# Weight sums in DRAM by smaller groups from the output projection on, later x forms, one gate block more in plain form, and another order of the second phase

## The chip, the core and the metric

One core of a Trainium2 chip runs the kernel. TensorE (PE; its weight loads are the row PEld), VectorE (DVE), ScalarE (ACT), GpSimd (POOL) and SyncE (SP) work from instruction queues of their own, each in its own order, and wait for one another at semaphores. SP, ACT and POOL also issue DMA transfers. The metric is the device time of one execution in microseconds, the median of several runs.

## What is computed

One layer on x of 512 tokens by 1024 features, in float32:

```python
h = rms_norm(x, norm_mix_g)
cb, cc, cin, q, k, v, f_logit, g_logit = split(h @ w_in)
y_conv = (cb * causal_dwconv(cc * cin, conv_mix_w)) @ w_out_conv
y_attn = forgetting_attention(q, k, v, cumsum(log_sigmoid(f_logit + b_f))) @ w_out_attn
g_conv, g_attn = split(sigmoid(g_logit + b_gate))
x = x + (g_conv * y_conv + g_attn * y_attn) @ w_o
a, b = split(causal_dwconv(rms_norm(x, norm_ffn_g) @ w_up, conv_ffn_w))   # 2816 wide each
x = x + (silu(a) * b) @ w_down
return rms_norm(x, norm_f_g)
```

## The kernel before

Features lie on the 128 partitions and tokens along the free axis, so x is 8 blocks (kb) of 128 by 512. Each weight chunk is 128 by up to 1024: eight 128x128 tiles, one per block of the contraction. To keep float32 accuracy, each operand is split into a high part, rounded to the PE's format (ACT, L250, names wh_...), and the low rest (DVE, L254, names wl_...). A product is three passes: high x high, low x high, high x low (mm3, L281). A plain block, one output block of 128 features, is 8 tiles x 3 passes x 2 halves of the tokens = 48 matmuls.

**Chunks and queues.** `stream` lists all weight chunks in the order of their use. `load` issues a chunk's DMA on SP into one of four buffers (`raw`; further ones for F chunks), a few chunks ahead; `split` makes the two parts, in two buffers of each kind; `chunk` hands them to the matmuls. A buffer is loaded again once its last split is done, so SP's queue runs some blocks ahead of PE. Small pieces of work wait in the list `later`, each with a chunk number from which it may run and a cost in us; `run_later`, at the end of every `split`, issues as many as a budget for the chunk allows, and `flush` forces those that a matmul is about to need.

**Seven-product steps.** For the gate weights of blocks j from GJ on, and for most of the down projection, 2x2 groups of tiles are multiplied with seven products in place of eight (`seven`, matmuls at L299). A step (i, q) is a pair of output blocks i and a pair of contraction blocks q. Two steps make a double, listed in GATES (gates) and STEPS (down projection, first and second phase). A double has 2 x 7 x 3 = 42 matmuls and two chunks: P with six tiles that are read as they are, F with eight tiles that are sums of weights. The input side needs sums too: `x_sums` and `x_split` make those of x for the gates (tiles xt, xth, xtl), the closures t13, t24 and hl in `glu` those of the hidden layer (tiles ge, go, gh, gl).

**Weight sums in DRAM.** The sums for F are made by DMA alone, from one DRAM tensor (`wst`) to a DRAM tile f, for a group of doubles at a time (`make_forms`). Six operations in a chain per group: a plain copy (SP, L194), an accumulating copy (POOL, L197), a copy of a part of f (SP), an accumulating copy (POOL), again a copy (SP) and an accumulating copy (POOL). A copy from f waits for the sum before it. `GROUPS` gives for each of the three sets the doubles per group, the slots between two operations of a chain, and the slots by which the next group's chain is shifted. A slot is a call of `slot()`: one per unit of attention, and one per up block; there `todo_bg` operations that are due are issued, and so take their place in SP's and POOL's queues between the loads and the vector work that are issued there.

**Order of the program.** v projection; q and k; attention units mixed with the remaining projections (here the gates' sums are made); then for each j of 8 the two gates and the mix block (conv and attention output); output projection wo0 to wo7; first phase: 24 up blocks (pairs j = 0 to 11, each evacuated by DVE and ACT and multiplied on POOL, L1026 and L1033), then the 12 doubles of STEPS[0]; second phase: 20 up blocks and the doubles of STEPS[1]; at last two output blocks in plain form (chunks dp0 to dp2, tile pdA and others) and the final norm. In the second phase i = 2 goes on in PSUM from the first phase (HELD), i = 0 takes the banks X and i = 1 the banks Y, which i = 2 holds before. The pair q = 10 comes from the last up blocks.

Of the kernel before, what the change touches and what calls it, by code (L numbers as in the profile page):

```python
# [10 lines left out]
AF = mybir.ActivationFunctionType  # L11
# [23 lines left out]
G1, G2, GF, BG, CM, CF, BF = 0, 8, 16, 24, 40, 52, 184  # L35
# [10 lines left out]
STEPS = (  # L46
    tuple(((i, q), (i, q + 1)) for i, q in ((0, 0), (0, 2), (1, 0), (1, 2), (0, 4), (1, 4)))
    + tuple(((i, q), (i, q + 1)) for i in (3, 2) for q in (0, 2, 4)),
    (((2, 6), (2, 7)), ((2, 8), (2, 9)), ((2, 10), (0, 6)), ((0, 7), (0, 8)), ((0, 9), (0, 10)))
    + (((1, 6), (1, 7)), ((1, 8), (1, 9)), ((1, 10),)),  # L50
)
HELD = 2

GJ = 2
GATES = tuple(((j, q), (j, q + 1)) for j in range(GJ, KB) for q in (0, 2))

PLAIN = [(m, k) for m in (6, 7) for k in range(*PHASES[1])]
PCUTS = (0, 8, 12, 20)

DOUBLES = GATES + STEPS[0] + STEPS[1]  # L60
GROUPS = {"gate": (2, 4, 1), 0: (4, 2, 4), 1: (4, 2, 3)}


@with_exitstack
def block_kernel(ctx, tc, xT, vecs, wv, win, wmix, wo, wup, wst, wdp, outT):
# [3 lines left out]
    nc = tc.nc  # L69
# [6 lines left out]
    def keep(ins):  # L76
        return tc.keep_in_program_order(ins)
# [16 lines left out]
    def col(i):  # L94
        return vec[:, i : i + 1]
# [22 lines left out]
    stream = [(f"v{kb}", wv[kb], S + H) for kb in range(KB)]  # L118
    stream += [wi(i) for i in early + late]
    n = 0  # L120

    def step_chunks(n):
        m = len(DOUBLES[n])
        return [(f"P{n}", wst[n, :, : 3 * m * P], 3 * m * P), (f"F{n}", n, 4 * m * P)]

    for j in range(KB):
        if j >= GJ:
            stream += step_chunks(n) + step_chunks(n + 1)
# [13 lines left out]
    raws, parts, order = [], [], {}  # L142
    pools = {"raw": wp}
    later = []
# [33 lines left out]
    def make_forms(n0, n1, key):  # L178

        size, step, shift = GROUPS[key]  # L180
        cuts = [n0]
        for n in range(n0 + 1, n1 + 1):
            if n == n1 or n - cuts[-1] == size or len(DOUBLES[n]) != len(DOUBLES[cuts[-1]]):
                cuts.append(n)
        for g, (a, b) in enumerate(zip(cuts, cuts[1:])):
            m = len(DOUBLES[a]) * P
            f = dr.tile([P, b - a, 4 * m], F32, tag=f"f{a}", name=f"f{a}")
            w = wst[a:b].rearrange("n p c -> p n c")
            x0, x1, x2 = w[:, :, 3 * m : 5 * m], w[:, :, 5 * m : 7 * m], w[:, :, 7 * m : 8 * m]
            for n in range(a, b):  # L190
                made[n] = f[:, n - a, :]

            def put(dst, src):
                return lambda: keep(nc.sync.dma_start(dst, src))  # L194

            def add(dst, src):
                return lambda: keep(nc.gpsimd.dma_start(dst, src, accum_op=ALU.add))  # L197

            f0, f1, f2 = f[:, :, : 2 * m], f[:, :, 2 * m : 3 * m], f[:, :, 3 * m :]
            ops = (put(f0, x0), add(f0, x1), put(f1, f[:, :, :m]), add(f1, x1[:, :, m:]), put(f2, f1), add(f2, x2))  # L200
            todo_bg.extend((make_forms.slot + step * k + shift * g, op) for k, op in enumerate(ops))
        todo_bg.sort(key=lambda w: w[0])

    make_forms.slot = 0

    def slot():

        while todo_bg and todo_bg[0][0] <= make_forms.slot:
            todo_bg.pop(0)[1]()
        make_forms.slot += 1  # L210
# [20 lines left out]
    def split(hl=None):  # L231

        k = len(parts)
        if k == len(stream):
            return
        nm, _, ncol = stream[k]
        load(k + (LOOK if len(raws) > KB else AHEAD))
        if hl is None:
            hl = []
            for x in "hl":  # L240
                if k == 0:
                    wp.tile([P, PADW[x]], F32, tag=f"pad{x}", name=f"pad_{x}")
                hl.append(wp.tile([P, D], F32R, tag=f"w{x}", name=f"w{x}_{nm}", bufs=2)[:, :ncol])
        hi, lo = hl
        raw = raws[k]
        if k == 0:
            for cs in (slice(0, VW), slice(VW, S + H)):
                keep(nc.vector.tensor_copy(hi[:, cs], raw[:, cs]))
        else:
            ins = nc.scalar.activation(hi, raw, AF.Copy)  # L250
            order["hi"] = ins.ins
            if k < KB:
                keep(ins)
        ins = nc.vector.tensor_sub(lo, raw, hi.bitcast(F32))  # L254
        order["lo"] = ins.ins
        if k < KB:
            keep(ins)
        held[tag_of(k)] -= 1
        parts.append((hi, lo))
        run_later(k, {"u": 1.7, "P": 1.6, "F": 0.75, "i": 3.0, "m": 3.0}.get(nm[0], 3.5))  # L260
# [380 lines left out]
    n = 4 * H  # L641
# [62 lines left out]
    for idx in late:  # L704
        kind, i = divmod(idx, 4)
# [7 lines left out]
    n = len(units)  # L713
# [22 lines left out]
    th = [slice(0, 2 * P), slice(2 * P, S)]  # L736

    def split_next():
        if len(parts) == chunk.n and not stream[chunk.n][0].startswith("dp"):
            split()  # L740

    open_ = {}
# [41 lines left out]
    xt = xp.tile([P, KB, S], F32, tag="x1", name="xt")  # L784
# [23 lines left out]

    for q in range(4):
        nc.gpsimd.dma_start(xt[:, 2 * q : 2 * q + 2, :], xT[:, 2 * q : 2 * q + 2, :])  # L810
        for kb in (2 * q, 2 * q + 1):
            nc.scalar.activation(xt[:, kb, :], xt[:, kb, :], AF.Copy, scale=col(G1 + kb))
    xq = xt.rearrange("p (q b) (h c) -> p q (b h) c", b=2, h=2)
    xqh, xql = (t.rearrange("p (q b) (h c) -> p q (b h) c", b=2, h=2) for t in (xth, xtl))

    def x_sums(qs):
        b11, b12, b21, b22 = (xq[:, qs, i, :] for i in range(4))

        def f():
            nc.vector.tensor_sub(b11, b11, b12)  # L820
            nc.vector.tensor_sub(b12, b22, b12)

        def g():
            nc.vector.scalar_tensor_tensor(b22, b11, -1.0, b22, op0=ALU.mult, op1=ALU.subtract)
            nc.vector.scalar_tensor_tensor(b21, b22, -1.0, b21, op0=ALU.mult, op1=ALU.subtract)

        return f, g
# [5 lines left out]

        return f

    k = [c[0] for c in stream].index("mix0")
    for q in (0, 2):
        f, g = x_sums(slice(q, q + 2))
        later.append((k, 1.4, (("q", q),), f))
        later.append((k, 1.5, (("q", q),), g))  # L840
        for i in (q, q + 1):
            later.append((k + 1, 1.25, (("q", i),), x_split(i)))
        k += 2
# [49 lines left out]
    for j in range(KB):  # L893
        gs = []
        if j == 0:
            evac_gate(0, gs)(gp[0])
            evac_gate(8, gs)(gp[1])
        elif j < GJ:
            run_all(proj(20 + j, f"ga{j}", evac_gate(j, gs), acc))
            run_all(proj(28 + j, f"gb{j}", evac_gate(8 + j, gs), acc))  # L900
        else:
            if j == GJ:
                acc = ring(2, 7, 3, 4)
            seven(GATES[2 * (j - GJ) : 2 * (j - GJ) + 2], 2 * (j - GJ), {j: (0, 1, 5, 6)}, gate_form, done=gate_pair(j, gs))
        wh, wl = chunk(f"mix{j}")
        yc, ya = acc(f"yc{j}"), acc(f"ya{j}")
        for pp, hh, ll, o in ((yc, ych, ycl, 0), (ya, oth, otl, 4)):
            for k in range(4):
                ks = slice((o + k) * P, (o + k + 1) * P)
                mm3(pp, wh[:, ks], wl[:, ks], hh[:, k, :], ll[:, k, :], k == 0, k == 3)  # L910
        if j >= GJ:
            split_next()
# [57 lines left out]
        return q  # L970

    po = None
    for j in range(KB):
        if j == 0:
            po = lead(["wo0", "wo1"], mh, ml)
        p = po[j] if j < 2 else block(f"wo{j}", mh, ml)
        xr = mt(f"xr{j}")
        nc.gpsimd.dma_start(xr, xT[:, j, :])
        nc.vector.tensor_add(x1[:, j, :], p, xr)
        nc.scalar.activation(x1h[:, j, :], x1[:, j, :], AF.Copy, scale=col(G2 + j))  # L980
        nc.vector.scalar_tensor_tensor(
            x1l[:, j, :], x1[:, j, :], col(G2 + j), x1h.bitcast(F32)[:, j, :],
            op0=ALU.mult, op1=ALU.subtract,
        )
        square_into(ssq2, x1[:, j, :], j == 0, mp, f"sq2_{j}")
# [126 lines left out]
    for ph, (j0, j1) in enumerate(PHASES):  # L1112
        if ph:
            flush()
            acc = ring(*X)
        n = len(GATES) + ph * len(STEPS[0])
        make_forms(n, n + len(STEPS[ph]), ph)
        for j in range(j0, j1):
            pu = None
            if j == 0:  # L1120
                nrm = {}

                def mid():
                    nrm["c"] = rstd_col([ssq2], NT, 6, "n2")

                def late():
                    nrm["b"] = rstd_sb(rstd_bc(nrm["c"], NT, 7, "n2"), "n2")

                pu = lead(["up0", "up1"], x1h, x1l, mid, late)
            glu(ph, j, up(j, nrm["b"], pu))  # L1130
        assert not todo_bg
        seven(
            STEPS[ph], len(GATES) + ph * len(STEPS[0]), ({0: X, 1: Y, 3: X, 2: Y}, {0: X, 1: Y, 2: Y})[ph],
            lambda q, g: (gh[:, place(ph, q) + g, :], gl[:, place(ph, q) + g, :]),
            goes_on=HELD if ph == 1 else None, stays=HELD if ph == 0 else None,
            done=lambda i, banks, ids: combine(ph, i, banks, ids),
        )
# [175 lines left out]
```

## Time and profile before

| | us |
|---|---|
| median of three runs | 737.57 (732.33 to 738.46) |
| the profiled execution | 735.92 |
| its span, first to last instruction | 734.1 |
| PE busy in it | 705.7 |
| DVE, ACT, POOL busy | 498.0, 338.5, 163.9 |
| mean granted PE clock | 0.984 |

The profile gives each engine's busy time, a list of who waited for whom (idle time of an engine, put down to what released it last), and busy times in any stretch of the span, with the clock that PE was granted there and the share of time that the 16 DMA engines were busy. Lines such as L250 belong to the helpers, so tiles tell the places apart: p_up is an up block, dn a seven-product step, p_ga and p_gb the two gates in plain form. In the table the span of one execution stands beside that execution's own time; the sums of the prediction are made against the latter.

### The profile page before, as it was taken

To read this page: it belongs to the slowest core of one execution; us is meant where nothing else is said; L and a number is where in the kernel's file an instruction comes from. 1 tells how busy PE (TensorE), PEld (TensorE's weight loads), DVE (VectorE), ACT (ScalarE), POOL (GpSimd) and SP (SyncE) were. 2 spreads that over 40 slices of the span, in tenths; PEclk is the share of its full clock that TensorE was granted. 3 is DMA by queue.
4 is the path that set the end of the run, shared out by engine and by line. 5 is a ranking of instruction groups with operands and counts; after the bars stand their busy time and mean duration, and the time that the engine had idled before them with its cause. 6 is when DMAs were issued, how large, how long until landed. Compare 5 with 4: busy or idle time off the path is not lost. (4 is left out here: it accounts for less than half of the span.)

```text
span 734.1 us, 14600 instructions
## 1 busy us (share of the span) xinstructions
PE 705.7 (96%) x6042; PEld 700.8 (95%) x6042; DVE 498.0 (68%) x773; ACT 338.5 (46%) x528; POOL 163.9 (22%) x177
## 2 busy tenths in 40 slices
PE   9999999999898999999999798999999999999996
PEld 9999999999898999999998698999999999998985
DVE  6687767556288778844385485877684687878683
ACT  6574545434455444434253243445443344445552
POOL 5124856522100000222222032210000213210002
PEclk9999999999999999999999989999999999999998
DMA  7428989542523555452447986774656489554313
GB/s 264 145 69 283 233 220 194 129 87 65 208 60 122 187 188 178 144 171 89 144 74 209 264 150 185 213 214 150 193 163 215 76 227 251 148 174 153 98 30 114
DMA packets 54130, 118.91 MB, mean 162 GB/s; under 512 B 4624, under 2 KB 24080, under 8 KB 54064
## 3 DMA queue, kind: packets, MB, share of 16 engines
q1 hardware_dynamic: 38320, 96.00, 40.5%
q0 software_dynamic: 14336, 20.75, 16.4%
q10 hardware_dynamic: 1408, 1.24, 0.5%
q8 instruction: 47, 0.77, 0.4%
q14 instruction: 19, 0.16, 0.1%
HBM read 115.80 MB, written 35.13 MB: 206 GB/s over the span
## 5 line engine op out<-in xcount | busy, mean ns | idle before, releaser
L281 PE MATMUL p_up<-x1h,wh_up 128*128 128x256 f32 x536 | 105.8, 279 | 0.0
L281 PE MATMUL p_up<-x1h,wl_up 128*128 128x256 f32 x536 | 105.7, 279 | 0.0
L281 PE MATMUL p_up<-x1l,wh_up 128*128 128x256 f32 x536 | 105.3, 278 | 0.0
L250 ACT ACTIVATE wh_up<-raw_up 128x1024 fp32r<-128x1024 f32 x44 | 46.6, 1058 | 96.8 <-PE p_up L281 54.6
L254 DVE TENSOR_TENSOR wl_up<-raw_up,wh_up 128x1024 fp32r<-128x1024 f32 x44 | 55.6, 1264 | 42.6 <-ACT wh_up L250 42.6
L281 PEld LDWEIGHTS p_up<-x1h,wh_up 128*128 128x128 f32 x536 | 82.1, 191 | 0.0
L281 PEld LDWEIGHTS p_up<-x1h,wl_up 128*128 128x128 f32 x536 | 82.1, 190 | 0.0
L281 PEld LDWEIGHTS p_up<-x1l,wh_up 128*128 128x128 f32 x536 | 81.7, 190 | 0.0
L1026 POOL TENSOR_TENSOR ge<-fu,fu 128x512 f32<-128x512 f32 x11 | 17.0, 1550 | 194.9 <-DVE fu L531 182.0
L281 PE MATMUL p_in<-xgh,wh_in 128*128 128x256 f32 x288 | 56.9, 279 | 1.0 <-ACT wh_in L250 1.0
L281 PE MATMUL p_in<-xgl,wh_in 128*128 128x256 f32 x288 | 56.5, 277 | 0.0
L281 PE MATMUL p_in<-xgh,wl_in 128*128 128x256 f32 x288 | 56.4, 277 | 0.0
L254 DVE TENSOR_TENSOR wl_F<-raw_F,wh_F 128x1024 fp32r<-128x1024 f32 (+1 forms) x32 | 43.7, 1365 | 14.8 <-ACT wh_F L250 14.8
L299 PE MATMUL p_up<-x1h,wh_up 128*128 128x256 f32 x168 | 41.4, 282 | 10.2 <-ACT wh_up L250 10.2
L250 ACT ACTIVATE wh_F<-raw_F 128x1024 fp32r<-128x1024 f32 (+1 forms) x32 | 33.7, 1052 | 32.9 <-PE dn L299 26.6
L197 POOL DMA_DIRECT2D f<-in_wst_dram x36 | 47.3, 1436 | 0.1
L1013 DVE TENSOR_TENSOR fz<-p_up,rb_n 128x512 f32<-128x512 f32 x44 | 30.2, 689 | 24.6 <-PE p_up L281 24.6
L281 PEld LDWEIGHTS p_in<-xgh,wh_in 128*128 128x128 f32 x288 | 44.7, 188 | 1.9 <-ACT wh_in L250 1.2
L281 PEld LDWEIGHTS p_in<-xgl,wh_in 128*128 128x128 f32 x288 | 43.6, 188 | 0.0
L281 PEld LDWEIGHTS p_in<-xgh,wl_in 128*128 128x128 f32 x288 | 43.5, 188 | 0.0
L299 PEld LDWEIGHTS p_up<-x1h,wh_up 128*128 128x128 f32 x168 | 32.1, 191 | 10.8 <-ACT wh_up L250 10.8
L250 ACT ACTIVATE wh_P<-raw_P 128x768 fp32r<-128x768 f32 (+1 forms) x32 | 26.6, 832 | 31.1 <-PE dn L299 22.7
(306 smaller groups left out, 2079.8 us busy)
## 6 DMA issues: line engine op xcount, KB each, us to landing
raw_up<-in_wup_dram SPq DMA_DIRECT2D x44, 512.0 KB, 5.6
raw_F<-f SPq DMA_DIRECT2D x31, 512.0 KB, 4.3
raw_in<-in_win_dram SPq DMA_DIRECT2D x24, 512.0 KB, 3.6
raw_P<-in_wst_dram SPq DMA_DIRECT2D x31, 384.0 KB, 4.2
f<-in_wst_dram POOLq DMA_DIRECT2D x14, 512.0 KB, 8.8
raw_mix<-in_wmix_dram SPq DMA_DIRECT2D x8, 512.0 KB, 6.6
raw_wo<-in_wo_dram SPq DMA_DIRECT2D x8, 512.0 KB, 4.1
f<-in_wst_dram SPq DMA_DIRECT2D x4, 1024.0 KB, 5.9
```

What stands on the lines that cost most here:

```text
L197: return lambda: keep(nc.gpsimd.dma_start(dst, src, accum_op=ALU.add))
L250: ins = nc.scalar.activation(hi, raw, AF.Copy)
L254: ins = nc.vector.tensor_sub(lo, raw, hi.bitcast(F32))
L281: keep(nc.tensor.matmul(out[:, cs], w, x[:, cs], start=start and i == 0 and c == 0, stop=stop and i == 2 and c == len(cut) - 1,))
L299: keep(nc.tensor.matmul(out, wl if x == 1 else wh, xl if x == 2 else xh, start=opens and bk not in seen, stop=closes and bk not in left,))
L1013: nc.vector.tensor_mul(z, p, rb2)
L1026: keep(nc.gpsimd.tensor_mul(ge, a.rearrange(halves_of, h=2), b.rearrange(halves_of, h=2)))
```

## The change

- **GROUPS** gives the two phases groups of two doubles. First phase: four slots between operations in place of two, a shift of one in place of four. Second phase: three in place of two, a shift of one in place of three. Chains: six for three in the first phase, five for three in the second.
- The first phase's chains start with the output projection, which now calls `slot()` too: eight slots more. The slot count starts at 0 with every call of `make_forms`.
- **x forms**: the scaling of x by the norm's weight (ACT) was issued right behind the DMAs of x, ahead of everything that followed; it is now put in `later`, to run from the split of the chunk mix1 on, and the sums likewise from mix1 in place of mix0.
- **GJ = 3**: the gates of block 2 are computed in plain form (two plain blocks of 48 matmuls in place of two doubles of 42), and there are ten gate doubles in place of twelve.
- **STEPS[1]**, the second phase's order: the pair of steps with (2, 10) comes one double later, and the single step moves from the end to the sixth place.
- `split_next` may also split dp0 ahead.

```diff
-    (((2, 6), (2, 7)), ((2, 8), (2, 9)), ((2, 10), (0, 6)), ((0, 7), (0, 8)), ((0, 9), (0, 10)))
-    + (((1, 6), (1, 7)), ((1, 8), (1, 9)), ((1, 10),)),
+    (((2, 6), (2, 7)), ((2, 8), (2, 9)), ((0, 6), (0, 7)), ((0, 8), (2, 10)), ((0, 9), (0, 10)))
+    + (((1, 6),), ((1, 7), (1, 8)), ((1, 9), (1, 10))),
...
-GJ = 2
+GJ = 3
...
-GROUPS = {"gate": (2, 4, 1), 0: (4, 2, 4), 1: (4, 2, 3)}
+GROUPS = {"gate": (2, 4, 1), 0: (2, 4, 1), 1: (2, 3, 1)}
...
     def make_forms(n0, n1, key):
 
         size, step, shift = GROUPS[key]
+        make_forms.slot = 0
...
-    make_forms.slot = 0
...
     def split_next():
-        if len(parts) == chunk.n and not stream[chunk.n][0].startswith("dp"):
+        if len(parts) == chunk.n and stream[chunk.n][0] not in ("dp1", "dp2"):
             split()
...
     for q in range(4):
         nc.gpsimd.dma_start(xt[:, 2 * q : 2 * q + 2, :], xT[:, 2 * q : 2 * q + 2, :])
-        for kb in (2 * q, 2 * q + 1):
-            nc.scalar.activation(xt[:, kb, :], xt[:, kb, :], AF.Copy, scale=col(G1 + kb))
...
+    def x_scale(q):
+        def f():
+            for kb in (2 * q, 2 * q + 1):
+                nc.scalar.activation(xt[:, kb, :], xt[:, kb, :], AF.Copy, scale=col(G1 + kb))
+
+        return f
...
-    k = [c[0] for c in stream].index("mix0")
+    k = [c[0] for c in stream].index("mix1")
     for q in (0, 2):
         f, g = x_sums(slice(q, q + 2))
+        for i in (q, q + 1):
+            later.append((k, 0, (("q", i),), x_scale(i)))
         later.append((k, 1.4, (("q", q),), f))
...
     po = None
+    make_forms(len(GATES), len(GATES) + len(STEPS[0]), 0)
     for j in range(KB):
+        slot()
         if j == 0:
             po = lead(["wo0", "wo1"], mh, ml)
...
         if ph:
             flush()
             acc = ring(*X)
-        n = len(GATES) + ph * len(STEPS[0])
-        make_forms(n, n + len(STEPS[ph]), ph)
+        if ph:
+            make_forms(len(GATES) + len(STEPS[0]), len(DOUBLES), ph)
```

**ACT at the gates.** ACT's queue from the last projection of the attention stage on: g are the gates' sigmoids, wh_in29 the split of the second gate's chunk of block 1, xt the scaling of x (L812 before, L816 now), xth the forms' high part. Before:

```order
L802 ACTIVATE g0_2609<-g0_2609,vec_64 128x512
L802 ACTIVATE g8_2612<-g8_2612,vec_64 128x512
L812 ACTIVATE xt_2589<-xt_2589,vec_64 128x512 x4
L250 ACTIVATE wh_in29_2725<-raw_in29_2392 128x1024
L812 ACTIVATE xt_2589<-xt_2589,vec_64 128x512 x4
```

And now:

```order
L801 ACTIVATE g0_2594<-g0_2594,vec_64 128x512
L801 ACTIVATE g8_2597<-g8_2597,vec_64 128x512
L249 ACTIVATE wh_in29_2706<-raw_in29_2385 128x1024
L924 ACTIVATE mh_2588<-g0_2594 128x512
L249 ACTIVATE wh_mix1_2712<-raw_mix1_2476 128x1024
L816 ACTIVATE xt_2582<-xt_2582,vec_64 128x512 x4
L801 ACTIVATE g1_2724<-g1_2724,vec_64 128x512
L249 ACTIVATE wh_in22_2780<-raw_in22_2545 128x1024
L835 ACTIVATE xth_2583<-xt_2582 128x1024 x2
```

The eight scalings moved from ahead of and around the split of in29 to behind the split of mix1 (four of them) and, not shown, behind that of in30.

**SP in the first up blocks.** SP's queue at the start of the first phase: raw_up are the up chunks' loads, f<-in_wst_dram a chain's first copy, f<-f a copy that waits for a sum. Before:

```order
L170 DMA raw_up4_4503<-in_wup_dram 128x1024
L194 DMA f12_4494<-in_wst_dram 512x1x512
L170 DMA raw_up5_4640<-in_wup_dram 128x1024
L170 DMA raw_up6_4701<-in_wup_dram 128x1024
L194 DMA f12_4494<-f12_4494 512x256
L194 DMA f16_4495<-in_wst_dram 512x1x512
L170 DMA raw_up7_4767<-in_wup_dram 128x1024
```

And now:

```order
L170 DMA raw_up4_4499<-in_wup_dram 128x1024
L195 DMA f10_3972<-f10_3972 256x256
L195 DMA f12_3973<-f12_3973 256x256
L195 DMA f14_3974<-f14_3974 256x256
L170 DMA raw_up5_4639<-in_wup_dram 128x1024
L195 DMA f16_3975<-f16_3975 256x256
L170 DMA raw_up6_4701<-in_wup_dram 128x1024
L195 DMA f18_3976<-f18_3976 256x256
L170 DMA raw_up7_4767<-in_wup_dram 128x1024
```

The first copies have left this place for the output projection; the copies from f are half as large, and one stands between two loads.

**DVE at the start of the second phase's steps.** wl_P26 and wl_F26 before, wl_P25 and wl_F25 now, are the low parts of the chunks of the double that holds (2, 10); go10 and gl are the sums of q = 10 and their low parts. Before:

```order
L254 TENSOR_TENSOR wl_P26_8237<-raw_P26_8052,wh_P26_8236 128x768
L1047 SCALAR_TENSOR_TENSOR go10_8120<-go10_8120 128x256
L1053 TENSOR_TENSOR gl_4492<-ge10_7983,gh_4491 128x2x256
L1048 SCALAR_TENSOR_TENSOR go10_8120<-go10_8120 128x256
L1053 TENSOR_TENSOR gl_4492<-go10_8120,gh_4491 128x512 x2
L254 TENSOR_TENSOR wl_F26_8275<-raw_F26_8054,wh_F26_8274 128x1024
L1053 TENSOR_TENSOR gl_4492<-go10_8120,gh_4491 128x512
```

And now:

```order
L253 TENSOR_TENSOR wl_P24_8255<-raw_P24_8070,wh_P24_8254 128x768
L1055 SCALAR_TENSOR_TENSOR go10_8138<-go10_8138 128x256
L1061 TENSOR_TENSOR gl_4491<-ge10_7999,gh_4490 128x2x256
L1056 SCALAR_TENSOR_TENSOR go10_8138<-go10_8138 128x256
L253 TENSOR_TENSOR wl_F24_8287<-raw_F24_8072,wh_F24_8286 128x1024
L1061 TENSOR_TENSOR gl_4491<-go10_8138,gh_4490 128x512
L253 TENSOR_TENSOR wl_P25_8319<-raw_P25_8139,wh_P25_8318 128x768
L1061 TENSOR_TENSOR gl_4491<-go10_8138,gh_4490 128x512 x2
L253 TENSOR_TENSOR wl_F25_8347<-raw_F25_8141,wh_F25_8346 128x1024
```

The three low parts of go10 stood behind the P chunk of the double that needs them; now one stands ahead of that chunk, and a whole double (P24, F24) that does not need them lies before.

## The prediction

> **What bounds the kernel now.** I read the busy times first, then what TensorE (PE) waits for, then stretches of 15 us, then the queues behind the waits. On the page:
>
> ```profile
> PE 705.7 (96%) x6042; PEld 700.8 (95%) x6042; DVE 498.0 (68%) x773; ACT 338.5 (46%) x528; POOL 163.9 (22%) x177
> ```
>
> PE is busy 96% of the span, so only two things can be gained: matmuls, and the few stretches in which PE stands still or runs slowly. The list of PE's waits names nearly all of the standing still (line; released by; us, times, longest):
>
> ```profile
> PE p_up L299 <- ACT wh_up L250: 10.2, 3, 5.5
> PE p_gb L281 <- ACT wh_in L250: 2.1, 1, 2.1
> PE pdA L281 <- DVE wl_dp L254: 1.6, 2, 0.8
> PE dn L299 <- DVE gl L1053: 1.4, 1, 1.4
> PE dn L299 <- ACT xth L831: 1.2, 1, 1.2
> PE dn L299 <- DVE xtl L832: 1.0, 2, 0.9
> PE p_gb L281 <- DVE wl_in L254: 0.8, 1, 0.8
> ```
>
> The stretches give the places and a second loss, the clock (columns: stretch, length, busy us and count of PE, PEld, DVE, ACT, POOL, then PE clock, DMA share, GB/s):
>
> ```profile
> 195.00:210.00 15.00, 12.14 (x93) 11.74 (x92) 8.31 (x10) 9.55 (x13) 1.21 (x1) 0.89 0.55 186
> 210.00:225.00 15.00, 12.33 (x101) 11.57 (x100) 12.56 (x15) 7.68 (x9) 1.29 (x1) 1.00 0.28 87
> 240.00:255.00 15.00, 15.00 (x134) 15.00 (x134) 11.86 (x16) 7.08 (x9) 1.30 (x1) 1.00 0.49 156
> 390.00:405.00 15.00, 13.22 (x113) 12.82 (x112) 9.84 (x13) 6.58 (x9) 3.92 (x3) 1.00 0.64 173
> 405.00:420.00 15.00, 11.51 (x102) 11.31 (x100) 6.82 (x13) 3.25 (x5) 1.30 (x1) 1.00 0.92 251
> 420.00:435.00 15.00, 13.00 (x91) 13.00 (x92) 10.96 (x14) 6.69 (x9) 5.59 (x5) 0.77 0.71 161
> 435.00:450.00 15.00, 12.01 (x106) 11.81 (x106) 6.24 (x11) 4.71 (x7) 0.79 (x1) 1.00 0.93 256
> 450.00:465.00 15.00, 14.95 (x117) 14.74 (x116) 12.44 (x19) 6.21 (x10) 5.18 (x4) 0.89 0.56 97
> 675.00:690.00 15.00, 13.37 (x98) 12.77 (x97) 9.94 (x16) 5.96 (x8) 0.00 (x0) 0.89 0.42 125
> ```
>
> The row at 240 is the undisturbed case: 134 matmuls in 15 us, 0.112 us each, so a plain block of 48 takes 5.4 us. The other rows fall into three places: the gates (195 to 225), the first up blocks (390 to 465) and the second phase's steps (675 to 690). Cut finely, the clock is at half in four pieces of about 3.4 or 6.8 us, each beginning during or just after an idle stretch:
>
> ```profile
> 202.40:205.90 3.50, 3.06 (x15) 3.06 (x16) 3.43 (x6) 3.05 (x5) 0.00 (x0) 0.52 0.48 150
> 420.90:427.70 6.80, 5.70 (x27) 5.70 (x28) 5.72 (x7) 4.37 (x6) 2.43 (x3) 0.51 0.38 150
> 451.50:455.00 3.50, 3.50 (x19) 3.50 (x18) 3.50 (x6) 1.43 (x2) 2.08 (x2) 0.51 0.00 1
> 680.20:683.70 3.50, 3.50 (x19) 3.50 (x18) 0.96 (x1) 0.84 (x1) 0.00 (x0) 0.51 0.40 150
> ```
>
> **The DRAM sums (up stage).** One of the three stalls there, in order of time (start, length):
>
> ```profile
> 398.86 2.37 POOL L197 DMA_DIRECT2D f<-in_wst_dram  x2
> 405.24 6.73 SPq L194 DMA_DIRECT2D f<-f  x2
> 412.75 2.54 SPq L170 DMA_DIRECT2D raw_up<-in_wup_dram  x4
> 420.89 1.06 ACT L250 ACTIVATE wh_up<-raw_up 128x1024 fp32r<-128x1024 f32 x1 [8.04 <-DMA raw_up<-in_wup_dram]
> 422.00 0.58 PE L299 MATMUL p_up<-x1h,wh_up 128*128 128x256 f32 x1 [5.49 <-ACT wh_up L250]
> ```
>
> POOL issues two sums, SP has come to the copies that read them and stands, and four loads of up weights stand behind the copies. When SP is free the loads go out together, the first lands too late, ACT cannot split it, PE idles 5.49 us. SP's own waits by stage say how the grouping matters; the rows are those of 40 to 180 us (gates: two doubles a group, four slots between a sum and its copy), 340 to 480 (first phase: four doubles, two slots) and 560 to 680 (second phase, the same), then PE in 560 to 665:
>
> ```profile
> SPq L194 <- DMA f<-in_wst_dram: 21.5, 9, 4.3
> ```
> ```profile
> SPq L194 <- DMA f<-in_wst_dram: 87.6, 6, 20.9
> ```
> ```profile
> SPq L194 <- DMA f<-in_wst_dram: 52.9, 6, 18.3
> ```
> ```profile
> 560.00:665.00 105.00, 105.00 (x929) 105.00 (x928) 76.72 (x108) 45.88 (x64) 22.00 (x18) 1.00 0.68 177
> ```
>
> The change gives both phases groups of two. In the first, spacing goes from two slots to four. A slot is one up block, 5.4 us, so a copy has 10.8 us more; and its sum is half as large:
>
> ```profile
> f<-in_wst_dram POOLq DMA_DIRECT2D x14, 512.0 KB, 8.8
> f<-in_wst_dram POOLq DMA_DIRECT2D x4, 1024.0 KB, 11.2
> L197 POOL DMA_DIRECT2D f<-in_wst_dram x36 | 47.3, 1436 | 0.1
> ```
>
> Landing falls by 11.2 - 8.8 = 2.4 us. Mean hold now 87.6 / 6 = 14.6 us; then 14.6 - 10.8 - 2.4 = 1.4. Longest now 20.9, then 7.7. The second phase shows what SP can bear: holds of 52.9 / 6 = 8.8 on average, 18.3 at most, and PE busy 105.00 of 105.00 us. So 7.7 should hide behind the four loaded buffers. The second phase itself gets three slots for two and smaller sums, so shorter holds than those that already cost nothing, though ten copies for six. The first six plain copies move ahead into the output projection; they read only inputs, so SP does not stand on them, and their traffic falls where eight blocks of PE work run. Nine more sums on POOL (36 to 45) cost 9 x 1.44 = 13 us of an engine at 22%; the products of the up blocks queue behind them there, and the copies and loads are what would wait for it. Hidden: 0; uncovered, one smallest stall (1.72 us, below).
> Worth: idle 1.78 + 3.49 + 2.00 + 2.99 + 0.05 = 10.3 (15 less PE's column from 390 to 465); clock 0.23 x 15 + 0.11 x 15 = 5.1, less 0.55 for half of the 1.1 us in which PE was idle in the slow piece: 4.6. **Term: -14.9.**
>
> **The x forms (gates).**
>
> ```profile
> 197.42 1.34 ACT L812 ACTIVATE xt<-xt,vec 128x512 f32<-128x512 f32 x2 [5.46 <-DMA xt<-in_xT_dram]
> 200.49 1.04 ACT L250 ACTIVATE wh_in<-raw_in 128x1024 fp32r<-128x1024 f32 x1
> 201.58 0.50 PE L281 MATMUL p_gb<-xgh,wh_in 128*128 128x256 f32 x2 [2.10 <-ACT wh_in L250]
> ```
>
> ACT stands 5.46 us for x from DRAM with a weight split behind it; PE then idles 2.10 and 0.8, and again 1.2 and 1.0 at the first seven-product block, for xth and xtl. After the change the split of the second gate of block 1 stands ahead of all scaling, and the forms have the blocks mix 1, both gates of block 2 and mix 2 as cover, 4 x 5.4 = 21.6 us, where scaling takes 8 x 0.67 = 5.4 of ACT. If that cover is gone the 7.2 below comes back. Idle 2.86 + 2.67 = 5.5, clock 0.11 x 15 = 1.65. **Term: -7.2.** Price: block 2 is plain, 96 matmuls for 84, 12 x 0.112: **+1.3.** Its four double chunks give way to two full ones, so ACT, DVE and DMA lose work.
>
> **Second phase's order.** The wait on gl (1.4 us at 679) is for the sums of the last pair of up blocks, needed by the third double. Now they are first needed by the fourth, one double later: 42 x 0.112 = 4.7 us against 1.63 idle in 675 to 690. The lone single leaves the end, where its PE time was half; but i = 2 now ends one double before its banks are taken again, where it had two; four short vector steps have to free them inside 4.7 us: 0, and if they don't, what they lack of it. Idle 1.63, clock 1.65. **Term: -3.3.** At the plain tail PE waits 1.6 for two splits; the first is now covered by a full double's F part, the second is not: between 0 and -1.6, I take **-0.7**. That dp0 may be split by the look-ahead moves nothing by itself: 0.
>
> **Sum**, on the profiled execution's own 735.92 (span 734.1): 735.9 - 14.9 - 7.2 + 1.3 - 3.3 - 0.7 = 711.1. I add half of the smallest stall seen in the up stage,
>
> ```profile
> 394.03 0.38 PE L299 MATMUL p_up<-x1h,wh_up 128*128 128x256 f32 x1 [1.72 <-ACT wh_up L250]
> ```
>
> 0.9, for a copy that still comes early: **712.0 us**. The median shown is 737.57, 1.6 above that execution (732.33 to 738.46); the waits that go are those that can vary, so I do not carry the 1.6 over. Low bound: count matmuls in place of idle time. 74 are missing against 134 at the gates, 141 in the up stage, 36 at 675: 8.3, 15.8 and 4.0 us. With 1.6 at the tail: 735.9 - 29.7 + 1.3 = 707.5. Some records can be missing from a trace, so I keep the smaller terms.
>
> **Rivals.** (a) SP stays held: twice the copies, each wait shorter but more of them, and POOL still issues sums only after products that wait for DVE. Half of the up term stays: 711.1 + 7.4 = 718.5. Against it: the gates' holds, 4.3 at most with the same grouping.
> (b) The edits of order do not do what they say: the forms are late at their new place in the gates and again at the fourth double. 711.1 + 7.2 + 3.3 = 721.6. Against it: 21.6 and 4.7 us of cover.
> (c) The half-speed pieces have another cause than the gaps and stay. For it: 1.72 us idle at 392 drew none, while 1.4 at 679 did. Three pieces, 3 x 1.65: 716.1. (The Trainium skill, "TensorE: Matmul & The Clock Gate", section "Why this matters for your kernels", asks only that no gap exceed about 3 us; by that rule three of the four pieces would not come from their gaps, which are 2.1, 2.99 and 1.4 us. The trace differs: each follows its gap within about 2 us.)
> (d) Slower: SP's copies in the first phase, twelve for six, each hold the loads as the six do now. Price 14.9 / 6 = 2.5 us a copy; all twelve: 711.1 + 29.8 = 740.9. It decides from ten such copies on (24.8 / 2.5). For it: DMA at 0.92 of its time in 405 to 420. Against it: spacing and size, as above.
>
> **How the numbers follow.** Forecast 0.66, (a) 0.17, (b) 0.07, (c) 0.05, (d) 0.05. 708 to 721 holds the forecast, (a) and (c), and leaves out (b), (d) and some of the edges. A measurement of this kernel can tell about 1% from no change, here 7.4 us, so faster means below 730.2: all but (d) and a mix of (a) and (b). Faster 0.92, same 0.04, slower 0.04.
>
> **What would show it.** Right: the row PE p_up <- ACT wh_up is gone or under 2 us; SP's wait on f in the up stage falls from 87.6 to under 25 us; PE clock 1.00 in every stretch between the start and the tail; no waits of dn on xth, xtl or gl; 12 more matmuls in the gates. Wrong: bursts of four raw_up loads behind a copy, ACT idle for raw_up with several us; or new waits in the output projection, whose blocks have none now.

## The result, and the profile after

The changed kernel takes **709.08 us** (median of 4 runs, 708.67 to 709.53), the kernel before 738.02 beside it (median of 4, 732.33 to 738.53). The ratio is **0.9625, with a 95% interval of 0.9577 to 0.9673**. The profiled execution took 709.15 us, with a span of 707.1 and a granted clock of 0.997 (before: 735.92, 734.1, 0.984). The forecast was 712.0, in a range of 708 to 721.

The page of the kernel after, its first rows and its rows of the sums: 12 matmuls more, PE busy 99% of the span.

```profile
PE 696.6 (99%) x6054; PEld 694.6 (98%) x6054; DVE 494.6 (70%) x766; ACT 336.7 (48%) x525; POOL 174.0 (25%) x189
...
L198 POOL DMA_DIRECT2D f<-in_wst_dram x48 | 56.4, 1293 | 0.0
...
f<-in_wst_dram POOLq DMA_DIRECT2D x29, 256.0 KB, 5.7
...
f<-in_wst_dram POOLq DMA_DIRECT2D x14, 512.0 KB, 8.1
```

What PE waits for in the kernel after (line; released by; us, times, longest). All seven rows that the prediction quoted are gone or, at pdA, nearly so. One row is new, the wait on wh_F.

```profile
PE p_in L280 <- ACT wh_in L249: 1.1, 1, 1.1
PE warm L108 <- DVE ones L100: 1.0, 1, 1.0
PE dn L298 <- ACT wh_F L249: 0.8, 1, 0.8
PE pdA L280 <- DVE wl_dp L253: 0.3, 1, 0.3
```

The stretches of 15 us at the three places (gates, up blocks, second phase's steps; the columns are those of the prediction). PE is busy throughout at full clock, except at the new wait:

```profile
195.00:210.00 15.00, 15.00 (x135) 15.00 (x134) 11.05 (x12) 8.39 (x11) 1.30 (x1) 1.00 0.55 192
...
405.00:420.00 15.00, 15.00 (x135) 15.00 (x134) 10.40 (x17) 5.05 (x6) 4.71 (x4) 1.00 0.40 125
...
670.00:685.00 15.00, 14.14 (x121) 13.81 (x119) 13.15 (x21) 10.04 (x16) 0.00 (x0) 1.00 0.12 36
```

SP's waits on f at 340 to 480 us, and at 560 to 680:

```profile
SPq L195 <- DMA f<-in_wst_dram: 20.1, 8, 4.5
```
```profile
SPq L195 <- DMA f<-in_wst_dram: 35.8, 7, 9.4
```

In the up stage SP's hold (the time that it stands at a copy from f, with loads behind it) fell from 87.6 us over 6 waits to 20.1 over 8.

Where the 27.0 us of span went, by the starts of each stage's first matmul in the two traces (us):

| stage | before | after | difference | forecast |
|---|---|---|---|---|
| up to the first gate of block 1 | 193.88 | 194.40 | +0.52 | 0 |
| gates | 114.74 | 107.44 | -7.30 | -7.2 + 1.3 = -5.9 |
| output projection | 43.52 | 43.52 | 0 | 0 |
| first up blocks | 148.56 | 132.50 | -16.06 | -14.9 (+0.9) |
| first phase's steps | 57.12 | 57.12 | 0 | 0 |
| second up blocks | 108.80 | 108.80 | 0 | 0 |
| second phase's steps | 39.90 | 37.36 | -2.54 | -3.3 |
| plain tail, to the end of the span | 27.58 | 25.96 | -1.62 | -0.7 |

By place, the up stage gained 16 us, the gates 7, and the steps and the tail at the end 4. Two questions were open: which of the edits does it in each place, and whether the reason given for it is the cause.

### The profile page after: what moved, and what is told of

Read it like the earlier page. It is cut to its first block, busy times and chain, and to the rows that moved or that the text cites. A ratio compares the mean times of both kernels' runs of the same rounds, so it can differ in the third digit from the quotient of the medians.

```text
span 707.1 us, 14653 instructions
## 1 busy us (share of the span) xinstructions
PE 696.6 (99%) x6054; PEld 694.6 (98%) x6054; DVE 494.6 (70%) x766; ACT 336.7 (48%) x525; POOL 174.0 (25%) x189
## 5 line engine op out<-in xcount | busy, mean ns | idle before, releaser
L280 PE MATMUL p_up<-x1l,wh_up 128*128 128x256 f32 x536 | 104.5, 276 | 0.0
L280 PE MATMUL p_up<-x1h,wh_up 128*128 128x256 f32 x536 | 104.4, 276 | 0.0
L280 PEld LDWEIGHTS p_up<-x1h,wh_up 128*128 128x128 f32 x536 | 80.7, 188 | 0.0
L280 PEld LDWEIGHTS p_up<-x1h,wl_up 128*128 128x128 f32 x536 | 80.6, 188 | 0.0
L253 DVE TENSOR_TENSOR wl_up<-raw_up,wh_up 128x1024 fp32r<-128x1024 f32 x44 | 53.8, 1223 | 20.6 <-ACT wh_up L249 20.6
L280 PE MATMUL p_in<-xgh,wl_in 128*128 128x256 f32 x288 | 56.4, 277 | 0.0
L198 POOL DMA_DIRECT2D f<-in_wst_dram x48 | 56.4, 1293 | 0.0
L253 DVE TENSOR_TENSOR wl_F<-raw_F,wh_F 128x1024 fp32r<-128x1024 f32 (+1 forms) x30 | 40.4, 1346 | 14.3 <-ACT wh_F L249 14.3
L249 ACT ACTIVATE wh_F<-raw_F 128x1024 fp32r<-128x1024 f32 (+1 forms) x30 | 31.6, 1052 | 30.3 <-PE dn L298 25.9
L298 PE MATMUL p_up<-x1h,wh_up 128*128 128x256 f32 x168 | 40.3, 277 | 0.0
L298 PE MATMUL p_up<-x1l,wh_up 128*128 128x256 f32 x168 | 40.2, 276 | 0.0
L253 DVE TENSOR_TENSOR wl_in<-raw_in,wh_in 128x1024 fp32r<-128x1024 f32 x26 | 34.7, 1336 | 7.3 <-ACT wh_in L249 6.8
```

The source lines that it names most:

```text
L280: keep(nc.tensor.matmul(out[:, cs], w, x[:, cs], start=start and i == 0 and c == 0, stop=stop and i == 2 and c == len(cut) - 1,))
L298: keep(nc.tensor.matmul(out, wl if x == 1 else wh, xl if x == 2 else xh, start=opens and bk not in seen, stop=closes and bk not in left,))
```

## The experiments

Each ratio is against the kernel before, run on the same chip beside the experiment (its medians there lay between 735.4 and 738.2). Stage lengths are taken from the traces as in the table above.

**The up stage: do the sums do it, and alone?** The first run takes the kernel after and puts back the grouping and the start of the sums:

```diff
-GROUPS = {"gate": (2, 4, 1), 0: (2, 4, 1), 1: (2, 3, 1)}
+GROUPS = {"gate": (2, 4, 1), 0: (4, 2, 4), 1: (4, 2, 3)}
...
-    make_forms(len(GATES), len(GATES) + len(STEPS[0]), 0)
...
-        slot()
...
-        if ph:
-            make_forms(len(GATES) + len(STEPS[0]), len(DOUBLES), ph)
+        n = len(GATES) + ph * len(STEPS[0])
+        make_forms(n, n + len(STEPS[ph]), ph)
```

> The changed kernel with only the DRAM sums put back: groups of four doubles, two slots between operations, the first chain starting with the up blocks. Theory (SP stands behind copies that wait for big, close sums, and the up loads stand behind SP): the first up blocks take 148.6 us again in place of 132.5, so 709.1 + 16.1 = 725.2, and the waits PE p_up <- ACT wh_up and three slow-clock pieces come back. Rival (half or more of the up stage's gain came with the other edits, which shift the whole program against the sums): under 718.

Measured: 723.59 (721.40 to 726.04), ratio 0.9817 [0.9761, 0.9873]. The up stage takes 147.50 and nothing else moves. PE's wait and SP's hold at 340 to 480 us are back:

```profile
PE p_up L298 <- ACT wh_up L249: 10.6, 3, 6.1
```
```profile
SPq L195 <- DMA f<-in_wst_dram: 88.0, 6, 21.3
```

The second run is the kernel before with this edit alone.

```diff
-GROUPS = {"gate": (2, 4, 1), 0: (4, 2, 4), 1: (4, 2, 3)}
+GROUPS = {"gate": (2, 4, 1), 0: (2, 4, 1), 1: (2, 3, 1)}
...
+        make_forms.slot = 0
...
-    make_forms.slot = 0
...
+    make_forms(len(GATES), len(GATES) + len(STEPS[0]), 0)
...
+        slot()
...
-        n = len(GATES) + ph * len(STEPS[0])
-        make_forms(n, n + len(STEPS[ph]), ph)
+        if ph:
+            make_forms(len(GATES) + len(STEPS[0]), len(DOUBLES), ph)
```

> The kernel before with only the DRAM sums changed: groups of two, four and three slots, start at the output projection. Theory: the same 16.1 us, 738.0 - 16.1 = 721.9; the gates keep their waits (p_gb, xth, xtl) and the second phase its wait on gl. Rival (the parts only pay together): above 727.

Measured: 721.27 (720.91 to 722.42), ratio 0.9787 [0.9746, 0.9828]. The up stage takes 132.50, the length after; the gates (114.96) and the rest stay as before. The part stands for itself, and the parts add.

**Is it SP's queue, or the traffic?** The copies from f of the first phase go to POOL's queue, in the kernel before; bytes, groups and spacing stay. POOL issues the sum ahead of them itself, so they wait there, and no load of weights stands behind them.

```diff
+            def put_f(dst, src):
+                eng = nc.gpsimd if key == 0 else nc.sync
+                return lambda: keep(eng.dma_start(dst, src))
...
-            ops = (put(f0, x0), add(f0, x1), put(f1, f[:, :, :m]), add(f1, x1[:, :, m:]), put(f2, f1), add(f2, x2))
+            ops = (put(f0, x0), add(f0, x1), put_f(f1, f[:, :, :m]), add(f1, x1[:, :, m:]), put_f(f2, f1), add(f2, x2))
```

> The kernel before, with the first phase's copies from f issued on POOL's queue in place of SP's; groups, spacing, start and every byte moved stay. Theory (the harm is that up loads stand behind a copy on SP): the holds move to POOL, where only products wait that are not needed soon, the up loads go out in time, and the first up blocks fall from 148.6 to 132 to 135 us: 722 to 725. Rival (the harm is the traffic, 1 MB sums and copies that slow the loads): still about 148, 738.

Measured: 721.15 (718.86 to 724.18), ratio 0.9783 [0.9741, 0.9826]. The up stage takes 132.50: the whole loss is gone, with the same bytes. The up stage of this run, then of the kernel before, 345 to 480 us:

```profile
345.00:480.00 135.00, 135.00 (x1192) 135.00 (x1191) 94.12 (x134) 60.87 (x84) 35.11 (x29) 1.00 0.72 198
```
```profile
345.00:480.00 135.00, 124.69 (x1051) 123.70 (x1050) 83.35 (x116) 52.98 (x73) 28.52 (x22) 0.96 0.67 175
```

In the profiled execution the gates took 118.09, 3.3 us more than in the kernel before (the clock was 0.50 from 205 to 210 us there), and this execution, 724.18, is the longest of the four. In the up stage PE runs at 135.00 of 135.00 with more traffic per us (198 GB/s against 175). So what counts is what stands behind the waiting copy in its queue: POOL itself stands 15.0 us at copies from 340 to 480 us, and PE waits for nothing there.

**Size, spacing or early start?** The change did three things to the first phase's sums at once. Four runs part them. The shift between chains is 4 in three of them, as in the kernel before, and 1 in late_start. Groups of four, four slots (from the kernel after; size undone):

```diff
-GROUPS = {"gate": (2, 4, 1), 0: (2, 4, 1), 1: (2, 3, 1)}
+GROUPS = {"gate": (2, 4, 1), 0: (4, 4, 4), 1: (2, 3, 1)}
```

> The changed kernel with groups of four doubles in the first phase, four slots between operations, start at the output projection (shift 4). If spacing alone decides, the holds are 14.6 - 10.8 = 3.8 us on average and nothing stalls: 709. If the size of the sums and copies decides, stalls of 2 to 5 us come back in the up blocks: 713 to 722.

Measured: 708.82 (708.04 to 709.42), ratio 0.9626 [0.9597, 0.9654]; up stage 132.50. Then groups of two, two slots (spacing undone):

```diff
-GROUPS = {"gate": (2, 4, 1), 0: (2, 4, 1), 1: (2, 3, 1)}
+GROUPS = {"gate": (2, 4, 1), 0: (2, 2, 4), 1: (2, 3, 1)}
```

> The changed kernel with groups of two doubles but two slots between operations in the first phase (shift 4, start at the output projection). If spacing decides, holds are 14.6 - 2.4 = 12 us on average and the up blocks stall again: 714 to 725. If size decides: 709.

Measured: 718.26 (716.19 to 719.12), ratio 0.9750 [0.9717, 0.9783]; up stage 141.62. PE's wait is back, and SP's hold (340 to 480 us) is as long in all as in the kernel before:

```profile
PE p_up L298 <- ACT wh_up L249: 5.2, 4, 2.2
```
```profile
SPq L195 <- DMA f<-in_wst_dram: 103.0, 11, 19.1
```

Then the start in the up blocks as before, with three slots (early start undone):

```diff
-GROUPS = {"gate": (2, 4, 1), 0: (2, 4, 1), 1: (2, 3, 1)}
+GROUPS = {"gate": (2, 4, 1), 0: (2, 3, 1), 1: (2, 3, 1)}
...
-    make_forms(len(GATES), len(GATES) + len(STEPS[0]), 0)
...
-        slot()
...
-        if ph:
-            make_forms(len(GATES) + len(STEPS[0]), len(DOUBLES), ph)
+        n = len(GATES) + ph * len(STEPS[0])
+        make_forms(n, n + len(STEPS[ph]), ph)
```

> The changed kernel with the first phase's chains starting at the up blocks as before, groups of two, three slots, shift one (four slots would not end in time). If the early start matters, the first copies and sums crowd the first up blocks and stalls of 2 us or more come back: 712 or above. If it does not, holds of 14.6 - 5.4 - 2.4 = 6.8 us hide as the second phase's do: 709.

Measured: 708.74 (708.53 to 708.88), ratio 0.9625 [0.9597, 0.9652]; up stage 132.50. At last the kernel before with one number changed:

```diff
-GROUPS = {"gate": (2, 4, 1), 0: (4, 2, 4), 1: (4, 2, 3)}
+GROUPS = {"gate": (2, 4, 1), 0: (4, 3, 4), 1: (4, 2, 3)}
```

> The kernel before with one number changed: in the first phase three slots in place of two between the operations of a chain of sums, in groups of four doubles as before. Theory (what decides is the time between a sum and the copy that reads it): the mean hold of SP falls from 14.6 by one slot, 5.4 us, to about 9, the size that cost nothing in the second phase; most of the up stage's 16 us come back, 722 to 725, and the wait of p_up on wh_up is under 3 us. Rival (also the size of the groups or the early start is needed): the stage keeps half of its loss or more, 730 to 736.

Measured: 720.15 (719.93 to 722.10), ratio 0.9788 [0.9760, 0.9815]; up stage 132.50. **This one number is worth as much as the whole change to the sums** (only_sums: 0.9787). SP's hold in its up stage, 340 to 480 us:

```profile
SPq L194 <- DMA f<-in_wst_dram: 39.6, 6, 10.3
```

In order of the longest hold: 4.5 us (after), 7.8 (big_wide), 8.4 (late_start) and 10.3 (one_number) cost PE nothing; 19.1 (small_narrow) costs 9.1 us and 20.9 (before) costs 16.1. The longest hold alone does not decide, though: in the second up blocks of the kernel before one of 18.3 us, with 52.9 in all, cost nothing, against 87.6 in all in the first and 103.0 in small_narrow. Where the limit lies between these was not tried. Sums half as large and an early start are not needed once there are three slots or more; with two, smaller sums and an early start brought back less than half, 6.9 of 16.1 us, and no run parts these two.

**The gates.** Here the change moved the scaling of x and made block 2 plain. The kernel after with block 2 in seven-product form again, and the forms counted from mix0 again, one block earlier, so that they are there for it:

```diff
-GJ = 3
+GJ = 2
...
-    k = [c[0] for c in stream].index("mix1")
+    k = [c[0] for c in stream].index("mix0")
```

> The changed kernel with the gates of block 2 again in seven products (GJ = 2), the x forms still behind the splits, counted from mix0. Theory A (the place of the scaling is what paid, the plain block only costs its twelve matmuls): 709.1 - 1.4 = 707.7, no wait at the first seven-product block. Theory B (the plain block's time is the cover that the forms need): waits of dn on xth and xtl of 2 to 3 us with or without a slow-clock piece of 1.7: 710 to 713.

Measured: 716.15 (715.22 to 716.21), ratio 0.9712 [0.9672, 0.9752]; the gates take 114.04, against 114.74 before and 107.44 after. The wait of p_gb is gone, but the first double stalls at 213 to 223 us instead:

```profile
213.06 0.39 PE L298 MATMUL dn<-xgh,wh_P 128*128 128x256 f32 x1 [1.62 <-DVE g L921]
...
220.79 0.39 PE L298 MATMUL dn<-xth,wh_P 128*128 128x256 f32 x1 [2.07 <-ACT xth L835]
222.04 0.38 PE L298 MATMUL dn<-xtl,wh_P 128*128 128x256 f32 x1 [0.87 <-DVE xtl L836]
```

The clock falls as well: it is 0.50 from 224 to 227 us. x lands as late here as in the kernel before (9.7 us against 9.8), but that is not what the forms wait for: the last scaling ends at 208.3 us, and the sums stand in DVE's queue behind splits and gates until 219.6:

```profile
218.23 0.68 DVE L828 SCALAR_TENSOR_TENSOR xt<-xt 128x512 f32<-128x512 f32 x1
218.95 0.69 DVE L829 SCALAR_TENSOR_TENSOR xt<-xt 128x512 f32<-128x512 f32 x1
```

So the moved scaling without the plain block gains 0.7 us: it shifts the stall from the block before the forms' first use to the use itself. The other half alone, the plain block with the scaling where it was:

```diff
         nc.gpsimd.dma_start(xt[:, 2 * q : 2 * q + 2, :], xT[:, 2 * q : 2 * q + 2, :])
+        for kb in (2 * q, 2 * q + 1):
+            nc.scalar.activation(xt[:, kb, :], xt[:, kb, :], AF.Copy, scale=col(G1 + kb))
...
-        for i in (q, q + 1):
-            later.append((k, 0, (("q", i),), x_scale(i)))
```

> The kernel after, except that x is scaled on ACT right behind its transfers from DRAM, as in the kernel before; block 2 stays plain and the forms' sums stay from mix 1 on. Theory (the place of the scaling decides only the wait at the second gate of block 1): the waits of p_gb on wh_in and wl_in come back, 2.1 and 0.8 us, with or without a half-clock piece of 1.7 us; none of dn on xth or xtl, since the plain block 2 still covers the forms. 709.1 + 2.9 = 712.0, up to 713.7. Rival (the plain block 2 alone pays, the place of the scaling is worth nothing): 709 and no wait of p_gb. Second rival (place and cover hang together): waits of dn on xth or xtl as well, 714 and more.

Measured: 709.61 (708.87 to 709.80), ratio 0.9637 [0.9612, 0.9662]; the gates take 107.60 and p_gb has no wait. The theory missed, the first rival held: **beside the plain block, moving the scaling is worth nothing.** But why does PE not wait at p_gb now, with the scaling at its old place? ACT stands for x half as long (2.71 us against 5.46), since x lands sooner. The transfers of x, from 178 to 200 us, and ACT's first scaling, in the kernel before:

```profile
xt<-in_xT_dram POOLq DMA_DIRECT2D x4, 512.0 KB, 9.8
raw_F<-f SPq DMA_DIRECT2D x2, 512.0 KB, 9.2
raw_P<-in_wst_dram SPq DMA_DIRECT2D x2, 384.0 KB, 5.3
```

and in the run gj3_early (views of the DMA and of ACT):

```profile
xt<-in_xT_dram POOLq DMA_DIRECT2D x4, 512.0 KB, 6.5
```
```profile
195.36 2.65 ACT L811 ACTIVATE xt<-xt,vec 128x512 f32<-128x512 f32 x4 [2.71 <-DMA xt<-in_xT_dram]
197.91 1.04 ACT L249 ACTIVATE wh_in<-raw_in 128x1024 fp32r<-128x1024 f32 x1
```

x's transfers are issued from 189.1 us on in the kernel before. Three of block 2's four chunks (two F and a P, 1.4 MB) are issued between 188.6 and 189.9; with block 2 plain it is one chunk of 0.5 MB. The last run on the gates takes gj3_early and puts such a load back, 1 MB into the same buffers, and nothing else:

```diff
+    for n in range(2):
+        more = mp.tile([P, D], F32, tag="rg", name=f"more{n}", bufs=2)
+        keep(nc.sync.dma_start(more, wup[n]))
     for q in range(4):
         nc.gpsimd.dma_start(xt[:, 2 * q : 2 * q + 2, :], xT[:, 2 * q : 2 * q + 2, :])
```

> The kernel of the run gj3_early (x scaled right behind its transfers, block 2 plain) with two further transfers of 512 KB each on SP, just ahead of those of x, into the two buffers that the F chunks of block 2 filled there in the kernel before; nothing reads what they bring. All else stands in the same order. Theory (x came late because block 2's four chunks were loaded beside it, and the plain block 2 took that load away): x lands after about 9.8 us in place of 6.5, ACT idles for it some 5 us, and the waits of p_gb on wh_in and wl_in return, 2 to 3 us: 712 to 714. Rival (the load beside x is not what made it late): x lands after 6.5 us, no wait of p_gb, 709.6.

Measured: 712.25 (711.21 to 712.75), ratio 0.9677 [0.9645, 0.9708]; the gates take 110.29, 2.7 more than in gj3_early. x lands late again, ACT stands 5.14 us for it, and p_gb waits (views of the DMA, ACT and PE's waits):

```profile
xt<-in_xT_dram POOLq DMA_DIRECT2D x4, 512.0 KB, 9.2
```
```profile
197.33 1.34 ACT L814 ACTIVATE xt<-xt,vec 128x512 f32<-128x512 f32 x2 [5.14 <-DMA xt<-in_xT_dram]
```
```profile
PE p_gb L280 <- ACT wh_in L249: 1.5, 1, 1.5
...
PE p_gb L280 <- DVE wl_in L253: 0.8, 1, 0.8
```

The load beside x is what made it late. It accounts for 2.7 of the 7.1 us that the plain block gains (114.74 to 107.60). Could block 2 keep its seven products (12 matmuls fewer) if the forms were made faster? Half of x is scaled on POOL, the forms are counted from mix0 and given smaller costs, so that they run earlier, and the PSUM banks go in another order (the main lines of the edit):

```diff
-GJ = 3
+GJ = 2
...
-    acc = ring(3, 4, 5, 6, 0, 1, 2, 7)
+    acc = ring(3, 4, 5, 6, 2, 7)
...
-    k = [c[0] for c in stream].index("mix1")
...
+                nc.gpsimd.tensor_scalar(
+                    xt[:, kb, :], xt[:, kb, :], col(G1 + kb), 0.0, op0=ALU.mult, op1=ALU.add
+                )
...
+    k = [c[0] for c in stream].index("mix0")
...
-        later.append((k, 1.4, (("q", q),), f))
-        later.append((k, 1.5, (("q", q),), g))
+        later.append((k, 1.0, (("q", q),), f))
+        later.append((k, 1.0, (("q", q),), g))
...
-            later.append((k + 1, 1.25, (("q", i),), x_split(i)))
+            later.append((k + 1, 0.7, (("q", i),), x_split(i)))
...
-                acc = ring(2, 7, 3, 4)
+                acc = ring(3, 4, 2, 7)
```

> A candidate beyond the kernel after: block 2 of the gates with seven products as in the kernel before (12 matmuls fewer, 1.3 us), but the forms are made ahead of it in time: half of x is scaled on POOL in place of ACT, the forms have smaller costs and so run earlier, and the PSUM banks go round in another order. If that is enough, no wait at the first seven-product step: 709.1 - 1.3 = 707.8. If the forms are still late there, waits of dn on xth, xtl or the PSUM banks of 1 to 4 us: 709 to 713.

Measured: 712.17 (711.37 to 712.89), ratio 0.9675 [0.9650, 0.9701]; the gates take 109.69. The forms are in time, but the split of the F chunk now stands behind them on ACT, and PE waits for that. So this one is slower than the kernel after, not better.

```profile
216.45 0.38 PE L298 MATMUL dn<-xgh,wh_F 128*128 128x256 f32 x1 [2.79 <-ACT wh_F L249]
```

**The second phase's order** put back, in the kernel after:

```diff
-    (((2, 6), (2, 7)), ((2, 8), (2, 9)), ((0, 6), (0, 7)), ((0, 8), (2, 10)), ((0, 9), (0, 10)))
-    + (((1, 6),), ((1, 7), (1, 8)), ((1, 9), (1, 10))),
+    (((2, 6), (2, 7)), ((2, 8), (2, 9)), ((2, 10), (0, 6)), ((0, 7), (0, 8)), ((0, 9), (0, 10)))
+    + (((1, 6), (1, 7)), ((1, 8), (1, 9)), ((1, 10),)),
```

> The changed kernel with the second phase's old order. Theory: the wait on gl and its slow-clock piece come back, 2.5 us over the steps, and the plain tail, 1.6 us longer before, is longer again because a single double ends the steps: 709.1 + 4.1 = 713.2. Rival (the tail's 1.6 came from the shifted program, not from the order): 711.6.

Measured: 711.19 (710.72 to 713.39), ratio 0.9654 [0.9611, 0.9696]. The profiled span is 709.0 against 707.1: the steps take 38.16 (37.36 after), the tail 27.4 (25.96). Both waits are back. The half-speed piece is not, in this execution: PE's waits, and the stretch with the gap, at full clock, where the prediction's row of the kernel before (675 to 690) has 0.89.

```profile
PE pdA L280 <- DVE wl_dp L253: 1.6, 2, 0.8
PE dn L298 <- DVE gl L1061: 1.4, 1, 1.4
```
```profile
655.00:670.00 15.00, 14.15 (x124) 14.15 (x125) 10.21 (x15) 7.62 (x11) 0.00 (x0) 1.00 0.37 110
```

Another of the four executions took 713.39, with a mean clock of 0.993 in place of the 0.997 here, so the piece may have come in that one; there is no trace of it.

## Why the prediction was right, and where its steps were not

- **The sums in the up stage (-14.9): right in mechanism, 1.2 us short.** Measured 16.06. The idle and clock columns were summed over 390 to 465; the count of matmuls in the same rows, used for the low bound, gave 15.8 and was the better measure. SP's hold fell to 2.5 us on average, over the eight copies that waited, and 4.5 at most, where 1.4 and 7.7 were forecast. Of the two reasons given for it, 10.8 us more of spacing and sums that land 2.4 us sooner, the spacing is enough by itself, and one slot of 5.4 us would have done (one_number); smaller sums are neither needed (big_wide) nor enough (small_narrow).
- **That the early copies cost nothing (0): right.** The output projection takes 43.52 in both. The early start also gains nothing measurable (late_start).
- **The sums on POOL: a slip in the count.** The prediction had 36 to 45 sums; it is 48: five groups for the gates, six and five for the phases, three sums each. POOL's issuing grew by 56.4 - 47.3 = 9.1 us, where 13 were counted. Both are hidden; the total is not touched by it.
- **The second phase's sums (0): right.** 108.80 us in both, with the old grouping (undo_sums) too.
- **x forms (-7.2) and the plain block 2 (+1.3): the sum nearly right by luck, the step wrong.** Net -5.9 forecast, -7.30 measured. The prediction gave the whole gain to the moved scaling and took the plain block as its price. It is the other way round: the scaling moved alone is worth 0.7 (undo_gj), the plain block alone 7.1 (gj3_early, 107.60). It acts twice: its chunks no longer load beside x, so x lands 3.3 us sooner and the wait of p_gb does not arise, shown by adding a load (gj3_loads, +2.7); and it lies ahead of the first seven-product step as cover, which fits what comes of taking it away (undo_gj, 2.07 and 0.87 of waiting for the forms). That run brings the late x back too; its sums stood behind other work on DVE, not for x, but seven products in block 2 without the loads beside x were not tried. The prediction did name the plain block as part of the cover and said that the 7.2 would come back without it; 6.6 came back (undo_gj, 114.04 against 107.44). What it had wrong is the moved scaling as the cause. The prediction read "ACT stands 5.46 us for x" and did not ask why x came late; the row of x's landing and those of raw_F and raw_P stood in the trace. Of the size: a count of matmuls gave 8.3 - 1.3 = 7.0 net.
- **The order of the steps (-3.3): -2.54, for a wait of 0.83 that was not foreseen.** The prediction looked at the vector steps that free the banks of i = 2 and priced them at 0, which held. What came instead stands on ACT: the squares and scalings of the last norm for the two blocks of i = 2 (L1111 to L1116) stand ahead of the split of an F chunk. With the old order they stand ahead of one too (undo_order, that split at 669.50 us) and PE does not wait. But i = 2 now ends one double later, and the single step, with half the PE time of a double, lies just ahead; which of the two makes the split late was not parted:

```profile
669.27 0.83 ACT L249 ACTIVATE wh_P<-raw_P 128x768 fp32r<-128x768 f32 x1
670.01 0.62 ACT L1111 ACTIVATE ssq<-x 128x512 f32<-128x512 f32 x1
670.53 0.61 ACT L1114 ACTIVATE sq<-x 128x512 f32<-128x512 f32 x1
671.05 1.32 ACT L1116 ACTIVATE x<-x,vec 128x512 f32<-128x512 f32 x2
672.28 1.04 ACT L249 ACTIVATE wh_F<-raw_F 128x1024 fp32r<-128x1024 f32 x1
```

  Without that wait the term would have been met, but half of it, the clock's 1.65, is not a sure part of the gap: it was there in the kernel before, not in the trace of undo_order with the same gap. Apart from the clock the order is worth 1.9 to 2.3 us, steps and tail together (undo_order: spans 709.0 and 707.1; 0.80 in the steps and 1.46 in the tail).
- **The plain tail (-0.7): -1.62.** Both splits are covered, not the first alone: PE's waits at pdA fell from 1.6 to 0.3 us. This is the upper end that was named, -1.6. The order does it, since both waits are back in undo_order, which keeps the look-ahead for dp0.
- **The sum.** The terms gave 711.1; the 0.9 added for a copy that still comes early was not needed, since p_up has no wait left. With the counts of matmuls and the tail's upper end the text had 707.5, below the measured 709.08 by 1.6: of it 0.8 is the new wait and 0.5 the later first gate.
- **The rivals.** (a), SP held half as long, and (d), each copy holding the loads, did not come: twelve copies hold less in all than six did. What both describe is real, though: with two slots in place of four, eleven waits of 19.1 us at most cost 9.1 us (small_narrow). (b), forms late again at their new place, is what happens without the plain block (undo_gj). (c), half-speed pieces that stay, did not come: the clock is 1.00 in every stretch quoted.

## What to carry to other kernels

When a transfer that waits shares a queue with loads, set the wait's distance first: here one slot more between a sum and the copy that reads it gave the whole 16 us, and putting the copy in another queue did so too; smaller pieces did not replace distance. When an engine stands for a transfer, read what else was issued in the same few microseconds before moving the engine's work: here two loads fewer beside x removed a wait, where moving the scaling brought another in its place. And undo the halves of a part one by one, since a total that fits can rest on the wrong half.

## What the runs showed of the hardware that was not expected

- **A gap does not decide by its length alone whether the clock drops.** Gaps of 2.1 (p_gb) and 1.4 us (gl) in the kernel before were followed by half-speed pieces of about 3.4 us; the same gap of 1.4 us in undo_order, 1.52 and 0.76 in gj3_loads, and 2.79 in gj2_pool were followed by none. The row of gj2_pool right behind its gap:

```profile
216.00:219.00 3.00, 2.55 (x22) 2.55 (x23) 3.00 (x4) 1.13 (x2) 2.03 (x1) 1.00 0.00 0
```

  The clock differs from one execution of a kernel to the next, too: gj2_pool took 711.37 us at a mean clock of 0.996 in one and 712.89 at 0.993 in another. So a clock term read from one trace need not hold for the next.

  The Trainium skill, "TensorE: Matmul & The Clock Gate", section "Why this matters for your kernels", asks for no gap above about 3 us; the 1.4 and 2.1 in the kernel before lie below that and were followed by half-speed pieces all the same. What decides stays open; no run here was made for it.
- **1 MB more beside a 2 MB transfer delays it by 2.7 us**: x's four pieces landed after 9.2 us (median, gj3_loads) in place of 6.5 (gj3_early). The DMA engines are busy all the time from 192 to 195 us in gj3_loads:

```profile
192.00:195.00 3.00, 3.00 (x29) 3.00 (x28) 0.97 (x2) 0.19 (x1) 0.00 (x0) 1.00 1.02 378
```
